# A two-layer hybrid block on one core: tokens loaded as feature columns, a later rate exponential, a scheduler that puts layer-norm steps first, and accumulating transfers for eight weight rows of the hybrid output

## The chip, the cores and the metric

The kernel runs on one core of one Trainium2 chip. The metric is device time in microseconds; the time of a kernel is the median of its runs. A profile shows one execution. The engines are TensorE (PE, with its weight loads as PEld), VectorE (DVE), ScalarE (ACT), GpSimd (POOL) and SyncE (SP), which here only issues transfers.

## What is computed

The input is one sequence of 256 tokens with 1024 features, all in float32. Six sublayers follow each other, each with a scaled residual (alpha is the square root of 2) and a layer norm: a feed-forward network, a hybrid mixer (a gated delta rule branch and a state-space branch side by side), two more feed-forward networks, a sparse attention mixer (NSA), and a last feed-forward network.

```python
def swiglu(x, w_in, w_out):
    gate, up = jnp.split(x @ w_in, 2, axis=-1)
    return (jax.nn.silu(gate) * up) @ w_out

def hybrid_mixer(x, w_in, ..., w_out):
    proj = x @ w_in
    ...
    o_a = gdn_branch(...)          # uses g = -exp(a_log) * softplus(a_logit + dt_bias)
    o_b = ssd_branch(...)          # uses a = -exp(a_log), dt = softplus(dt_logit + dt_bias)
    return jnp.concatenate([o_a, o_b], axis=-1) @ w_out
```

A feed-forward network goes from 1024 to twice 2816 features and back, with half its output added to the residual. The hybrid output multiplies 2048 features (16 rows of 128) by a 2048 x 1024 matrix.

## The kernel before

**Products of split operands.** Every large product is made from two parts per operand. A high part is the value rounded to the fast matmul type (fp32r), a low part is what is left. `split` writes the high part with a copy (ACT, or DVE where the planner chooses) and the low part with a subtraction on DVE. Three matmuls give high by high, high by low and low by high. A weight tile of 128 x 1024 (512 KB) is loaded by SP into a tile `raw` and split into `whi` and `wlo` (`arrive`, `halved`). Tokens are held as feature columns: `x[0]` is four tiles with high and low parts, each for two blocks of 128 features and both blocks of 128 tokens; `x[1]` keeps the unsplit columns, from which `token_forms` builds the sums for the wide products.

**Added rows.** `rows(w, f, added)` loads one row tile of an output matrix. With `added`, the low part is not subtracted on DVE: ACT writes minus the rounded value into `wlo`, and a transfer issued by POOL adds the weights from memory on top. Before the change, seven of the 22 rows of each feed-forward output (`ADDED`) are made in this way and none of the hybrid output.

**The planner.** All operations are first recorded in a `Plan` with tiles and data dependencies. `order` then simulates the engines with a price per operation and a latency per pair of engines, and picks at each step, for each engine, the operation that can start first; ties go to the lower priority number, which is the order of recording. It decides the order of the instructions on each engine, and through it which buffer is used when. On the chip, engines run their lists in order and wait only for data and buffers. A gate (`_Gate`, `late`) is a dependency for the planner alone. Every instruction is emitted by one helper, so all of them have line 561 in the profile, and groups are told apart by tiles. 52 tiles of 4 KB per partition hold everything in SBUF, with quotas by stream; `ORDER` adds fixed random offsets to the priorities of the NSA stage, drawn with a fixed number.

**The start.** `run` spins TensorE on a tile of ones, loads the token rows in four parts (`load`), transposes each part on TensorE in four blocks, copies the transposed part into `x[1]` and splits it into `x[0]` (`transpose_half`). Parts two to four are loaded and transposed between the weight tiles of `first_weights`, as `arrivals` say. `first_steps` then multiplies the first 512 gate features (four weight tiles, bank `acc`, 48 matmuls) and the first 512 up features (four tiles, bank `ps`, 48 matmuls). The loaded rows stay in `self.ah` as the residual.

**The hybrid stage.** `hybrid` loads its small parameters early, behind a gate. `rate`, the exponential of the decay parameters, is recorded after the copy of the projected logits and before the sigmoid; it depends only on its own small load. Five generators (`delta`, `space`, `gate`, `space2`, `out_a`) are woven together. `out_a` multiplies rows 0 to 7 of the output matrix, and rows 8 to 15 follow in `out_terms`, which takes the last `LAG` = 7 rows first for all of token block 0 and then for block 1, so that the norm of block 0 runs beside the products of block 1.

**Layer norm.** `layer_norm` adds the residual, takes the statistics, normalises in two halves, and transposes and splits each half for the next stage.

Of the kernel before, what the change touches and what calls it, by code (L numbers as in the profile page):

```python
# [10 lines left out]
F32R = mybir.dt.float32r  # L11
# [7 lines left out]
P = 128  # L19
# [31 lines left out]
CHUNKS, AHEAD, LAG = 4, 3, 7  # L51

TERMS = ((0, 1, 1, 1, 1, 1, 1), (0, 0, 1, 1, 1, 1, 0), (0, 0, 1, 1, 1, 1, 0), (0, 0, 1, 1, 1, 0, 0))

ADDED = range(8, 22, 2)
# [6 lines left out]
RANK = 0  # L62

# [118 lines left out]
class Op:  # L182
    __slots__ = ("eng", "fn", "args", "kw", "idx", "prio", "cost", "table", "deps", "succ", "ndep", "ready", "start",
                 "end", "alloc", "dense", "alts", "tiles", "nbytes", "quad", "port", "banks")


class Plan:
# [11 lines left out]
    def __init__(self):  # L199
        self.ops = []  # L200
        self.tiles = []
        self.base = 0
        self.gate = None
        for e in ("tensor", "vector", "scalar", "gpsimd", "sync"):
            setattr(self, e, _Eng(self, e))
# [7 lines left out]
    def add(self, eng, fn, args, kw, alts=None):  # L213
        op = Op()
        op.eng, op.fn, op.args, op.kw, op.idx = eng, fn, args, kw, len(self.ops)
        op.prio = op.idx + self.base
        op.alts = alts
        op.deps, op.succ, op.alloc, op.nbytes = {}, [], None, 0
# [133 lines left out]
    def order(self, caps):  # L352
# [27 lines left out]
        port = 0.0  # L380
# [67 lines left out]
        while left:  # L448
            best = None
            for e in engs:  # L450
# [6 lines left out]
                for op in lst:  # L457
# [24 lines left out]
            (key, op, pen), e = best  # L482
            st = key[0] + pen
# [23 lines left out]
            if fn == "dma_start":  # L507

                at, need = st + 1300, op.nbytes * (2 if e == "gpsimd" else 1)
                while need > 0:  # L510
                    n = int(at / 500)
                    room = (155e3 if at < 8000.0 else 190e3) - moved.get(n, 0)
                    take = min(need, room, room * (n + 1 - at / 500), 95e3 if e == "gpsimd" else need)
# [3 lines left out]
                op.end = at + 600  # L517
# [67 lines left out]
class K:  # L585
    NT = 2
# [130 lines left out]
    def first_weights(self, w, n0, arrivals):  # L717

        out = []
        for n in range(4):  # L720
            src = w[n0 + n]
            raw = self.m4(1024, "raw", "W")
            hi, lo = (self.m4(1024, name, "W", F32R) for name in ("whi", "wlo"))
            step = 512 if arrivals and n < 2 else 1024
            for e in range(0, 1024, step):
                cs = slice(e, e + step)
                self.nc.sync.dma_start(raw[:, cs], src[:, cs])
                self.split(hi[:, cs], lo[:, cs], raw[:, cs])
                for f in (arrivals.pop(0) if arrivals else []):
                    f()  # L730
            out += [(hi[:, k * 512:k * 512 + 512], lo[:, k * 512:k * 512 + 512]) for k in range(2)]
        return out
# [207 lines left out]
    def layer_norm(self, b, acc, s, gb, x, last):  # L940
# [70 lines left out]
    def first_steps(self, x, w_in, gtiles, gts):  # L1011
# [4 lines left out]
        for c0, tag, arrivals in ((0, "acc", self.arrivals), (DFF, "ps", [])):  # L1016
# [15 lines left out]
        for b in range(2):  # L1032
# [6 lines left out]
            for f in range(4):  # L1039
                self.split(gts[f][0][:, b * P:(b + 1) * P], gts[f][1][:, b * P:(b + 1) * P], pt[:, f * P:(f + 1) * P])  # L1040
            with _Gate(self.plan, len(self.plan.ops) - 1):
                self.scale_h(b)

    def ffn(self, l, j, x, then, last=False):
# [5 lines left out]
        NT = self.NT  # L1050
# [21 lines left out]
        else:  # L1072
# [4 lines left out]
            for b in range(2):  # L1077
                for s in range(NT):
                    ps = self.bank("ps")
# [28 lines left out]
        steps = NF // 2 - 2 * CHUNKS  # L1108
        for s in range(NT, steps):
            wg, wu = (self.col_tiles([w_in[8 + 4 * (s - NT) + 2 * n + e] for e in range(2)]) for n in range(2))  # L1110
# [14 lines left out]
        for n in range(CHUNKS):  # L1125
            f0 = 2 * steps + 4 * n
            gout = [self.m4(1024, name, "G", F32R).rearrange("p (f t) -> p f t", f=4) for name in ("gh", "gl")]
            part = self.wide(w_in, 8 + 4 * (steps - NT) + 8 * n, forms, gout)
            for most in TERMS[n]:
# [119 lines left out]
    def hybrid(self, x, then):  # L1249
# [430 lines left out]
        def out_a():  # L1680
# [3 lines left out]
            for s in range(4):  # L1684
                wo = [self.rows(w_out, 2 * s + e) for e in range(2)]
# [9 lines left out]
        for s in range(4):  # L1695
            wo = [self.rows(w_out, 8 + 2 * s + e) for e in range(2)]
# [406 lines left out]
    def run(self, stages):  # L2103
# [14 lines left out]
        spin(4, 2)  # L2118
        self.ah = [self.m4(D, f"h{b}", "L") for b in range(2)]

        def load(b, q):
            cs = slice(q * 512, (q + 1) * 512)
            nc.sync.dma_start(self.ah[b][:, cs], self.i['x'][0, b * P:(b + 1) * P, cs])
            self.transpose_half(x, b, self.ah[b], q)

        load(0, 0)
        with _Gate(self.plan, len(self.plan.ops) - 3):
            spin(2, 2)
        self.arrivals = [[], [lambda: load(1, 0)], [], [lambda: load(0, 1), lambda: load(1, 1)]]
# [45 lines left out]
_INS = ['x', 'positions', 'ln_g', 'ln_b', 'ffn_w_in', 'ffn_w_out', 'hyb_w_tok', 'hyb_w_col', 'hyb_w_small',  # L2175
# [5 lines left out]
def laid_out(inputs):  # L2181
# [4 lines left out]
    steps = DFF // 256 - 2 * CHUNKS  # L2186
    ffn = []
    for l in range(2):
        for j in range(2):
            w = a['ffn_w_in'][l, j]  # L2190
            g, u = w[:, :DFF], w[:, DFF:]
            if l + j == 0:
                t = [rows(g[:, :512], 2), rows(u[:, :512], 2)]
            else:
                t = [rows(np.concatenate([g[:, c:c + 256], u[:, c:c + 256]], 1), 2) for c in (0, 256)]
# [43 lines left out]
```

## Time and profile before

| | us |
|---|---|
| median of 3 runs | 1088.05 (1086.9 to 1091.03) |
| the profiled execution | 1087.19 |
| its span, first to last instruction | 1085.5 |
| ACT busy | 725.9 |
| POOL busy | 70.7 |

The span is cut in stages by the order of the sublayers. In the page's picture of 40 slices (27.1 us each; digits are tenths of busy time) the four lines that matter are these:

```profile
PE   8999999998999999999999999999999999999997
...
DVE  7999999799979999999999999999978889999995
ACT  7767866368737774667866667678465778666780
...
PEclk9999999999999999999999999999999899999999
DMA  8658768535433575367777736679563336457881
```

PE and DVE are full in nearly all slices, ACT at two thirds, the DMA engines at a half to three quarters. The granted clock of TensorE is full but for one slice in the NSA stage. Where an engine waited, and for what, is shown with the prediction.

### The profile page before, as it was taken

Reading aid. Unit: us, or ns where it says so; the run is one execution under the profiler, and the core shown is the slowest. Engines: PE = TensorE matmul, PEld = TensorE weight load, DVE = VectorE, ACT = ScalarE, POOL = GpSimd, SP = SyncE. Lnnn points to the kernel's source line nnn. Section 1 sums busy time; section 2 is a strip of 40 time slices with the busy share of each in tenths; the row PEclk is TensorE's granted clock in tenths of the full one; section 3 lists DMA queues with packets and bytes.
Section 4 is the critical chain, followed back from the end, with each engine's and each line's share of the span. In section 5 each row is a group of like instructions: output and inputs, shape, how many; then the busy total and the mean of one; then the engine's idle time right before and its main releaser. Section 6 shows DMA issues by size and latency. Waiting matters only on the chain.

```text
span 1085.5 us, 16212 instructions
## 1 busy us (share of the span) xinstructions
PE 1066.3 (98%) x5946; PEld 893.3 (82%) x5946; DVE 1010.9 (93%) x1453; ACT 725.9 (67%) x1155; POOL 70.7 (7%) x116
## 2 busy tenths in 40 slices
PE   8999999998999999999999999999999999999997
PEld 6788888897999788888888888888887778888886
DVE  7999999799979999999999999999978889999995
ACT  7767866368737774667866667678465778666780
POOL 1000000001001310000000000000001000000000
PEclk9999999999999999999999999999999899999999
DMA  8658768535433575367777736679563336457881
GB/s 330 231 196 256 221 233 284 179 135 182 140 115 99 194 269 180 117 230 251 215 229 254 257 125 215 235 241 303 189 214 98 92 123 216 152 188 236 255 231 41
DMA packets 65034, 215.71 MB, mean 199 GB/s; under 512 B 8301, under 2 KB 12218, under 8 KB 64954
## 3 DMA queue, kind: packets, MB, share of 16 engines
q1 hardware_dynamic: 60922, 199.98, 52.8%
q0 software_dynamic: 4032, 14.68, 7.2%
q8 instruction: 47, 0.77, 0.3%
q14 instruction: 33, 0.27, 0.1%
HBM read 211.86 MB, written 1.07 MB: 196 GB/s over the span
## 4 chain that ended last, share of the span: by engine, by line
PE 84%; DVE 12%; ACT 1%; DMA 1%; issue 1%; POOL 0%; SPq 0%; DVEq 0%; ACTq 0%
PE ps L561 39%; PE acc L561 31%; PE mp L561 14%; DVE wlo L561 2%; DVE cv L561 2%; DVE arena L561 1%; DMA raw<-in_ffn_w_in_dram 1%; DVE o L561 1%; DVE sw L561 1%; DVE x L561 1%; DVE y L561 1%; DVE qs L561 1%; DVE AT L561 0%; POOL arena L561 0%; DVE Y L561 0%
## 5 line engine op out<-in xcount | busy, mean ns | idle before, releaser
L561 ACT ACTIVATE whi<-raw 128x1024 fp32r<-128x1024 f32 (+1 forms) x435 | 436.8, 1052 | 104.0 <-DVE raw L561 85.4
L561 DVE TENSOR_TENSOR wlo<-raw,whi 128x1024 fp32r<-128x1024 f32 (+2 forms) x419 | 491.4, 1205 | 7.1 <-ACT whi L561 6.1
L561 PE MATMUL ps<-whi,x 128*128 128x512 f32 (+1 forms) x864 | 234.8, 390 | 0.3 <-ACT cv L561 0.3
L561 PEld LDWEIGHTS ps<-whi,x 128*128 128x128 f32 x864 | 156.7, 188 | 30.6 <-issue 1.5
L561 DVE TENSOR_TENSOR raw<-raw,raw 128x1024 f32<-128x1024 f32 x128 | 152.8, 1216 | 0.0
L561 PE MATMUL ps<-wlo,x 128*128 128x512 f32 (+1 forms) x432 | 127.1, 385 | 0.0
L561 PE MATMUL ps<-x,whi 128*128 128x256 f32 (+2 forms) x560 | 114.3, 312 | 4.0 <-ACT cv L561 2.4
L561 PEld LDWEIGHTS ps<-x,whi 128*128 128x128 f32 (+1 forms) x560 | 90.4, 188 | 11.4 <-ACT cv L561 3.8
L561 PE MATMUL acc<-whi,gh 128*128 128x512 f32 x253 | 99.3, 393 | 0.0
L561 PE MATMUL acc<-wlo,gh 128*128 128x512 f32 x253 | 99.0, 391 | 0.0
L561 PE MATMUL acc<-whi,gl 128*128 128x512 f32 x253 | 97.9, 390 | 0.0
L561 PEld LDWEIGHTS ps<-wlo,x 128*128 128x128 f32 x432 | 79.6, 188 | 15.3 <-issue 0.4
L561 PE MATMUL ps<-x,wlo 128*128 128x256 f32 (+1 forms) x344 | 80.0, 284 | 0.5 <-DVE wlo L561 0.5
L561 PE MATMUL acc<-whi,x 128*128 128x512 f32 x224 | 73.7, 405 | 2.3 <-DVE x L561 0.8
L561 PE MATMUL acc<-whi,g 128*128 128x512 f32 x192 | 63.3, 392 | 0.0
L561 POOL DMA_DIRECT2D wlo<-in_ffn_w_out_dram x28 | 24.4, 872 | 569.2 <-ACT wlo L561 391.3
L561 PEld LDWEIGHTS ps<-x,wlo 128*128 128x128 f32 (+1 forms) x344 | 58.1, 189 | 2.1 <-DVE wlo L561 0.7
L561 PEld LDWEIGHTS acc<-whi,gl 128*128 128x128 f32 x253 | 47.5, 188 | 9.8
L561 PEld LDWEIGHTS acc<-whi,gh 128*128 128x128 f32 x253 | 47.5, 188 | 9.5
L561 PEld LDWEIGHTS acc<-wlo,gh 128*128 128x128 f32 x253 | 47.5, 188 | 9.5
L561 PEld LDWEIGHTS acc<-whi,x 128*128 128x128 f32 x224 | 41.8, 189 | 11.8 <-ACT whi L561 2.1
L561 PE MATMUL mp<-whi,fhi 128*128 128x512 f32 x128 | 49.9, 390 | 0.0
(284 smaller groups left out, 1735.2 us busy)
## 6 DMA issues: line engine op xcount, KB each, us to landing
raw<-in_ffn_w_in_dram SPq DMA_DIRECT2D x174, 512.0 KB, 5.5
raw<-in_ffn_w_out_dram SPq DMA_DIRECT2D x88, 512.0 KB, 3.7
wlo<-in_ffn_w_out_dram POOLq DMA_DIRECT2D x28, 512.0 KB, 8.5
raw<-in_hyb_w_col_dram SPq DMA_DIRECT2D x28, 512.0 KB, 4.5
raw<-in_hyb_w_tok_dram SPq DMA_DIRECT2D x16, 512.0 KB, 7.8
raw<-in_hyb_w_out_dram SPq DMA_DIRECT2D x16, 512.0 KB, 3.7
raw<-in_nsa_w_tok_dram SPq DMA_DIRECT2D x8, 512.0 KB, 6.6
raw<-in_nsa_w_one_dram SPq DMA_DIRECT2D x8, 512.0 KB, 5.8
```

Source lines behind the costliest of these rows:

```text
L561: r = getattr(getattr(nc, eng), fn)(*[res(a) for a in args], **{k: res(a) for k, a in kw.items()})
```

## The change

Seven things change.

1. **Tokens as feature columns.** The host passes the tokens a second time, transposed, as `x_cols`: four tiles, each of 128 partitions (the features of a block) by two token blocks, two feature blocks and 128 tokens. `first_loads` issues a column tile before each of the first four weight tiles and then the other four weight tiles; the columns go straight into `x[1]` and are split from there. The transposes, their copies and `arrivals` go. The token rows for the residual are loaded later, behind a gate on the last of these loads.
2. **Spin.** Two spins of 512 columns at the start in place of one of 512 and three of 256, the last two of which were behind a gate.
3. **Late exponential.** `rate` is recorded after the sigmoid and gated on the sigmoid's exponential.
4. **Layer norm first.** Operations recorded inside `layer_norm` are marked `hot`; on DVE and ACT the planner compares them as if they could start 135 ns earlier than they can.
5. **Added rows in the hybrid output.** The eight even rows of 16 get their low part by a transfer.
6. **The planner's model of accumulating transfers.** They follow each other, move up to 130 instead of 95 KB per half microsecond, and end 500 ns later.
7. **Chunks per feed-forward network.** `CHUNKS` becomes a tuple, with code for a fifth chunk; all four values are 4, as before.

```diff
-CHUNKS, AHEAD, LAG = 4, 3, 7
+CHUNKS, AHEAD, LAG = (4, 4, 4, 4), 3, 7
...
-ADDED = range(8, 22, 2)
+ADDED, ADDED_HYB = range(8, 22, 2), range(0, 16, 2)
...
+HOT = 135.0
+
+ADD_RATE, ADD_LATE = 130e3, 500.0
...
-                    key = (st if st > f + 1e-9 else f, p)
+                    at = st - HOT if op.hot and e in ("vector", "scalar") else st
+                    key = (at if at > f + 1e-9 else f, p)
                     if cand is None or key < cand[0]:
-                        cand = (key, op, pen)
+                        cand = (key, op, pen, st)
...
-            (key, op, pen), e = best
-            st = key[0] + pen
+            (key, op, pen, st), e = best
+            st = max(st, free[e]) + pen
...
                 at, need = st + 1300, op.nbytes * (2 if e == "gpsimd" else 1)
+                if e == "gpsimd":
+                    at = max(at, adds)
...
-                    take = min(need, room, room * (n + 1 - at / 500), 95e3 if e == "gpsimd" else need)
+                    take = min(need, room, room * (n + 1 - at / 500), ADD_RATE if e == "gpsimd" else need)
...
-                op.end = at + 600
+                if e == "gpsimd":
+                    adds = at
+                op.end = at + 600 + (ADD_LATE if e == "gpsimd" else 0.0)
...
+    def first_loads(self, x, w):
+
+        nc = self.nc
+        raws = []
+        for n in range(8):
+            if n < 4:
+                nc.sync.dma_start(x[1][n // 2][:, :, n % 2 * 2:n % 2 * 2 + 2, :],
+                                  self.i['x_cols'][n].rearrange("p (b k t) -> p b k t", b=2, k=2))
             raw = self.m4(1024, "raw", "W")
...
+            for cs in [slice(0, 512), slice(512, 1024)] if n == 0 else [slice(0, 1024)]:
+                nc.sync.dma_start(raw[:, cs], w[n][:, cs])
+            raws.append(raw)
+        return raws
...
-    def layer_norm(self, b, acc, s, gb, x, last):
+    def layer_norm(self, *args):
+        self.plan.hot = True
+        self.normalize(*args)
+        self.plan.hot = False
+
+    def normalize(self, b, acc, s, gb, x, last):
...
-            w = self.first_weights(w_in, 4 if c0 else 0, arrivals)
+            w = []
+            for n in range(4):
+                if c0 == 0:
+                    hi, lo = (x[0][n][:, :, e] for e in range(2))
+                    self.split(hi, lo, x[1][n // 2][:, :, n % 2 * 2:n % 2 * 2 + 2, :].rearrange("p b k t -> p k b t"))
+                w += self.first_weights(raws.pop(0), [slice(0, 1024)] if c0 or n else [slice(0, 512), slice(512, 1024)])
...
+            with self.late():
+                nc.sync.dma_start(self.ah[b], self.i['x'][0, b * P:(b + 1) * P])
             with _Gate(self.plan, len(self.plan.ops) - 1):
                 self.scale_h(b)
...
-        nc.scalar.activation(rate, rate, AF.Exp)
         beta = self.sm([P, 2, 8], "beta")
         self.sigmoid(beta, sm[:, :, 0:8])
+        with _Gate(self.plan, len(self.plan.ops) - 3):
+            nc.scalar.activation(rate, rate, AF.Exp)
...
-                wo = [self.rows(w_out, 2 * s + e) for e in range(2)]
+                wo = [self.rows(w_out, 2 * s + e, 2 * s + e in ADDED_HYB) for e in range(2)]
...
-            wo = [self.rows(w_out, 8 + 2 * s + e) for e in range(2)]
+            wo = [self.rows(w_out, 8 + 2 * s + e, 8 + 2 * s + e in ADDED_HYB) for e in range(2)]
...
-        spin(4, 2)
+        spin(4, 4)
...
+    a['x_cols'] = a['x'].reshape(2, P, 4, 2, P).transpose(2, 4, 0, 3, 1).reshape(4, P, 512)
```

More of the change, by code (lines that the diff above doesn't have):

```diff
@@ L183 @@
     __slots__ = ("eng", "fn", "args", "kw", "idx", "prio", "cost", "table", "deps", "succ", "ndep", "ready", "start",
-                 "end", "alloc", "dense", "alts", "tiles", "nbytes", "quad", "port", "banks")
+                 "end", "alloc", "dense", "alts", "tiles", "nbytes", "quad", "port", "banks", "hot")
 class Plan:
@@ L217, in add @@
         op.alts = alts
+        op.hot = self.hot
         op.deps, op.succ, op.alloc, op.nbytes = {}, [], None, 0
@@ L379, in order @@
         partial = False
-        port = 0.0
+        port = adds = 0.0
         activity = {}
@@ L585 @@
 class K:
-    NT = 2
     def __init__(self, plan, ins, caps):
@@ L715, in rows, with first_weights @@
         return hi, lo
[L717 to L721, printed above, removed]
-            raw = self.m4(1024, "raw", "W")
[L723 to L732, printed above, removed]
+    def first_loads(self, x, w):
[5 more added lines that the diff above has]
+                                  self.i['x_cols'][n].rearrange("p (b k t) -> p b k t", b=2, k=2))
+            raw = self.m4(1024, "raw", "W")
+            for cs in [slice(0, 512), slice(512, 1024)] if n == 0 else [slice(0, 1024)]:
+                nc.sync.dma_start(raw[:, cs], w[n][:, cs])
+            raws.append(raw)
+        return raws
+    def first_weights(self, raw, parts):
+        hi, lo = (self.m4(1024, name, "W", F32R) for name in ("whi", "wlo"))
+        for cs in parts:
+            self.split(hi[:, cs], lo[:, cs], raw[:, cs])
+        return [(hi[:, k * 512:k * 512 + 512], lo[:, k * 512:k * 512 + 512]) for k in range(2)]
     def token_forms(self, x):
@@ L1015, in first_steps @@
         banks = []
-        for c0, tag, arrivals in ((0, "acc", self.arrivals), (DFF, "ps", [])):
+        raws = self.first_loads(x, w_in)
+        self.mark = len(self.plan.ops) - 1
+        for c0, tag in ((0, "acc"), (DFF, "ps")):
             both = [self.bank(tag) for b in range(2)]
             banks.append(both)
-            w = self.first_weights(w_in, 4 if c0 else 0, arrivals)
+            w = []
[4 more added lines that the diff above has]
+                w += self.first_weights(raws.pop(0), [slice(0, 1024)] if c0 or n else [slice(0, 512), slice(512, 1024)])
             for k0 in range(0, KD, 2):
@@ L1049, in ffn @@
         NF = DFF // P
-        NT = self.NT
+        CH = CHUNKS[2 * l + j]
+        NT = 2 if CH < 5 else 1
         pairs = {}
@@ L1078, in ffn @@
                 for s in range(NT):
-                    ps = self.bank("ps")
+                    ps = self.bank("ps" if NT > 1 else "acc")
                     self.proj_tok(x, b, steps[s], ps)
@@ L1107, in ffn @@
         terms += [(f, gts[f]) for f in range(2 * NT)]
-        steps = NF // 2 - 2 * CHUNKS
+        steps = NF // 2 - 2 * CH
+        if steps == NT:
+            forms = self.token_forms(x)
         for s in range(NT, steps):
-            wg, wu = (self.col_tiles([w_in[8 + 4 * (s - NT) + 2 * n + e] for e in range(2)]) for n in range(2))
+            wg, wu = (self.col_tiles([w_in[4 * NT + 4 * (s - NT) + 2 * n + e] for e in range(2)]) for n in range(2))
             self.mark = len(self.plan.ops) - 1
@@ L1124, in ffn @@
         weights_to(AHEAD)
-        for n in range(CHUNKS):
+        for n in range(CH):
             f0 = 2 * steps + 4 * n
             gout = [self.m4(1024, name, "G", F32R).rearrange("p (f t) -> p f t", f=4) for name in ("gh", "gl")]
-            part = self.wide(w_in, 8 + 4 * (steps - NT) + 8 * n, forms, gout)
-            for most in TERMS[n]:
+            part = self.wide(w_in, 4 * NT + 4 * (steps - NT) + 8 * n, forms, gout)
+            for most in TERMS[CH][n]:
                 next(part)
@@ L2117, in run @@
         nc.scalar.activation(tab, self.mhalf, AF.Silu)
-        spin(4, 2)
+        spin(4, 4)
         self.ah = [self.m4(D, f"h{b}", "L") for b in range(2)]
[L2121 to L2129, printed above, removed]
         self.marks = []
@@ L2191, in laid_out @@
             g, u = w[:, :DFF], w[:, DFF:]
+            CH = CHUNKS[2 * l + j]
+            steps = DFF // 256 - 2 * CH
             if l + j == 0:
@@ L2194, in laid_out @@
             else:
-                t = [rows(np.concatenate([g[:, c:c + 256], u[:, c:c + 256]], 1), 2) for c in (0, 256)]
+                t = [rows(np.concatenate([g[:, c:c + 256], u[:, c:c + 256]], 1), 2) for c in ((0, 256) if CH < 5 else (0,))]
             for c in range(512, steps * 256, 256):
```

7 lines of the change are left out of this document (4 added, 3 removed).

## The prediction

> **What bounds the kernel now.** I read the page's busy times and its chain first, then the waits of TensorE by stretch, then tables by window. In all rows of windows the columns are stretch and its length, busy us (instructions) of PE, PEld, DVE, ACT and POOL, granted clock, DMA share, GB/s.
>
> ```profile
> PE 1066.3 (98%) x5946; PEld 893.3 (82%) x5946; DVE 1010.9 (93%) x1453; ACT 725.9 (67%) x1155; POOL 70.7 (7%) x116
> ...
> PE 84%; DVE 12%; ACT 1%; DMA 1%; issue 1%; POOL 0%; SPq 0%; DVEq 0%; ACTq 0%
> ```
>
> TensorE is busy for 1066.3 of 1085.5 us. No edit takes a matmul of the model away (only 16 transposes of the tokens go), so the change can win little more than the 19 us in which PE stands still. Where those lie is told by PE's waits, first for the stretch 0 to 50 us, then 200 to 400, then 400 to 1070 (columns: total us, times, longest):
>
> ```profile
> PE ps L561 <- DVE sg L561: 1.6, 2, 1.1
> PE acc L561 <- POOL ones L561: 1.1, 1, 1.1
> PE acc L561 <- DVE x L561: 0.8, 2, 0.6
> PE acc L561 <- ACT whi L561: 0.8, 1, 0.8
> PE acc L561 <- ACT x L561: 0.5, 1, 0.5
> ...
> PE ps L561 <- ACT cv L561: 2.7, 3, 1.3
> PE ps L561 <- DVE wlo L561: 0.5, 1, 0.5
> ...
> PE mp L561 <- DVE arena L561: 1.3, 2, 0.8
> PE mp L561 <- ACT arena L561: 0.8, 1, 0.8
> ```
>
> So there are four places: the start, the convolutions of the hybrid stage (waits on cv), a short stretch of the NSA stage (arena), and the tail. The chain shows the start in order of time (start, us, what):
>
> ```profile
> 12.71 8.89 PE acc L561 x39
> 21.60 7.27 PE ps L561 x32
> ...
> 29.37 7.09 DMA raw<-in_ffn_w_in_dram
> ...
> 52.09 2.72 PE acc L561 x12
> ```
>
> Twelve dense matmuls take 2.72 us (last row). The first group of the first feed-forward stage (bank acc, 48 matmuls, 10.9 us of work) ends only at 21.6: 39 of its matmuls run without a break from 12.7, and before that PE spends its time on warm-up matmuls, transposes and waits. Its inputs come in like this:
>
> ```profile
> 0.00:3.00 3.00, 1.94 (x3) 0.90 (x4) 0.34 (x2) 1.49 (x2) 2.18 (x13) 1.00 0.34 110
> 3.00:6.00 3.00, 2.35 (x8) 1.37 (x6) 1.12 (x4) 0.63 (x1) 1.29 (x7) 1.00 0.80 257
> 6.00:9.00 3.00, 2.14 (x9) 1.62 (x9) 1.59 (x3) 1.11 (x2) 0.00 (x0) 1.00 1.01 311
> 9.00:12.00 3.00, 2.24 (x13) 1.54 (x12) 0.94 (x3) 2.12 (x6) 0.00 (x0) 1.00 1.03 417
> ...
> 24.00:27.00 3.00, 3.00 (x15) 2.49 (x14) 3.00 (x3) 2.05 (x3) 0.00 (x0) 1.00 0.78 229
> 27.00:30.00 3.00, 3.00 (x15) 2.49 (x14) 3.00 (x5) 2.48 (x3) 0.00 (x0) 1.00 0.37 50
> ```
>
> By these rates 0.33, 1.10, 2.03 and 3.28 MB have come by 3, 6, 9 and 12 us.
>
> **The change part by part.** *Tokens first.* The group needs 1 MB of tokens and 2 MB of weights before as after, so the bytes do not change; their use does. Before, nothing of a token quarter can be multiplied until rows have landed, four transposes have run and PSUM has been read. After, quarter n (0.26 MB) and weight tile n (0.52 MB) come in turn, and PE can do 12 matmuls with each pair. Pair n is complete at 0.79, 1.57, 2.36 and 3.15 MB, which by the rates above is about 4.8, 7.5, 9.8 and 11.7 us. What lies between landing and matmul:
>
> ```profile
> 4.41 0.63 ACT L561 ACTIVATE whi<-raw 128x512 fp32r<-128x512 f32 x1 [2.10 <-DMA raw<-in_ffn_w_in_dram]
> 6.22 0.68 DVE L561 TENSOR_TENSOR wlo<-raw,whi 128x512 fp32r<-128x512 f32 x1
> ...
> L561 ACT ACTIVATE whi<-raw 128x1024 fp32r<-128x1024 f32 (+1 forms) x435 | 436.8, 1052 | 104.0 <-DVE raw L561 85.4
> L561 DVE TENSOR_TENSOR wlo<-raw,whi 128x1024 fp32r<-128x1024 f32 (+2 forms) x419 | 491.4, 1205 | 7.1 <-ACT whi L561 6.1
> ```
>
> A pair costs ACT 0.63 + 1.05 = 1.7 us and DVE 0.68 + 1.21 = 1.9, both under PE's 2.72. With 1.05 for ACT's high part and about half a microsecond to land and hand over, pairs 1 to 3 can start at 9.1, 11.4 and 13.3 us. Pair 0 starts near 5.4, when ACT's first half at 4.41 is through (its end and the hand-over), and waits for its second half as before, to about 9. Then PE is the limit: 9.1, 11.8, 14.5, end 17.2. Against 21.6 that is **-4.4 us**. If loads never held it, 5.4 + 10.9 = 16.3 gives -5.3; if each pair came 1 us later, -3.4. The runs of the token tiles in SBUF are 1 KB; the nearest rows are the 4 KB rows at 417 GB/s above and, for 512-byte runs of zero fills,
>
> ```profile
> 264.00:265.00 1.00, 1.00 (x9) 1.00 (x10) 1.00 (x4) 1.00 (x1) 0.00 (x0) 1.00 1.02 284
> ```
>
> At 284 the megabyte takes 3.7 us where at 311 it takes 3.4: nothing.
>
> Does the gain last? The token rows are now loaded a second time for the residual: two more transfers on SP's queue behind the eight weight tiles, ahead of or among the next weights (1 MB, 2.5 us at 417). The DMA has 0.22 + 0.63 of 3 us free between 24 and 30, 2.6 us, and that covers it. The weights of the row 29.37 are issued as PE frees buffers, so they move up with PE. VectorE was idle for 8.0 of the first 12 us (rows above) and is full afterwards; it gains most of that. I keep -4.4, but -2 as the lower end, in case DVE moves up by less than PE. The spin matmuls fill time in which PE waits for data either way: nothing.
>
> *Late exponential.* In ACT's timeline (start, us):
>
> ```profile
> 31.55 1.28 ACT L561 ACT_TABLE_LOAD   x1
> ...
> 42.96 1.28 ACT L561 ACT_TABLE_LOAD   x1
> ```
>
> The rate's Exp switches the table inside a Silu stretch and back: 2.6 us of ACT go, and in the hybrid stage the Exp sits beside another. PE runs through both, with half a microsecond of the wait on sg near the second. I take -0.2, bounds 0 and -0.5.
>
> *Layer norm first.* The windows with the first boundary, then those where the hybrid's output rows are multiplied, then the NSA stretch:
>
> ```profile
> 160.00:180.00 20.00, 20.00 (x94) 16.64 (x93) 19.04 (x22) 16.39 (x19) 1.09 (x2) 1.00 1.00 327
> 180.00:200.00 20.00, 20.00 (x97) 16.34 (x96) 19.67 (x38) 7.24 (x15) 2.00 (x2) 1.00 0.60 218
> ...
> 360.00:380.00 20.00, 19.34 (x96) 15.03 (x96) 19.60 (x47) 14.84 (x30) 10.62 (x21) 1.00 0.71 238
> 380.00:400.00 20.00, 19.83 (x108) 16.26 (x107) 19.56 (x30) 13.45 (x26) 2.59 (x1) 1.00 0.76 266
> ...
> 840.00:860.00 20.00, 17.65 (x101) 13.71 (x98) 17.02 (x42) 16.47 (x57) 1.51 (x5) 0.83 0.18 61
> ```
>
> PE is at 20.00 of 20 across the boundary: half of the output matmuls hide the norm of the other half. The head start of 135 ns makes DVE wait at most that long, or lets a norm step pass a 1.2 us split. 0, bounds -1 and +0.5.
>
> *Eight added rows.* DVE loses 8 x 1.21 = 9.6 us, ACT gains 8 x 1.05 = 8.4, POOL 8 issues, the DMA 4 MB more. PE's idle time between 360 and 400 is 0.66 + 0.17 us, so the relief is worth at most 0.8; I take **-0.4**. The other side is the latency. Rows on loads (the additions' queue: packets, MB, share of the 16 engines; the landing of its 28 transfers; this stage's plain rows, with their landing; SP's issues of the last seven of them; and in the chain the matmuls with the second eight):
>
> ```profile
> q0 software_dynamic: 4032, 14.68, 7.2%
> ...
> DMA to landing us min/median/max: 5.4/8.5/11.2
> ...
> raw<-in_hyb_w_out_dram SPq DMA_DIRECT2D x16, 512.0 KB, 3.7
> ...
> 371.03 15.40 SPq L561 DMA_DIRECT2D raw<-in_hyb_w_out_dram  x7
> ...
> 396.38 7.07 PE acc L561 x31
> ```
>
> An added row needs 3.7 + 1.05 + about 1 (hand-over and issue) + 8.5 = 14.3 us from issue to use, a subtracted one 3.7 + 1.05 + 1.2 = 6. SP issues its last rows near 385. The matmuls with the second eight begin near 396, and by the order in out_terms the last added row is first used after 27 of them, 6 us later, 17 us after its issue: covered by 3 us. On POOL, which works in order, the additions stand between the stage's selections and powers (10.62 us busy from 360 to 380): a power behind an addition waits for ACT's copy, and the output norm of the branch waits for it. The 28 transfers hold the engines for 78 us, 2.8 each; eight more in the 40 us at 0.71 and 0.76 fill those to the brim. If that costs, up to +2.
>
> *New planner constants.* They reorder every stage. Idle that could be won: 3.2 us in the hybrid (cv and wlo), 2.4 in NSA, and 0.17 of the clock over 20 us there, 3.4; any of it can also double. I take 0, bounds -4 and +3. CHUNKS keeps the value 4 everywhere, so its new code changes nothing.
>
> Sum: -4.4 - 0.2 - 0.4 = -5.0. The profiled execution took 1087.19, its span 1085.5; the median of the runs is 1088.05, within 0.1%. 1087.2 - 5.0 = **1082.2 us**.
>
> [...] Loads and additions compete; a window among the first stage's last additions and one after them:
>
> ```profile
> 163.00:166.00 3.00, 3.00 (x15) 2.49 (x14) 3.00 (x4) 3.00 (x4) 0.00 (x0) 1.00 1.02 279
> ...
> 190.00:193.00 3.00, 3.00 (x15) 2.47 (x14) 2.96 (x6) 0.00 (x0) 0.37 (x1) 1.00 1.03 418
> ```
>
> Full engines move 279 instead of 418 GB/s. [...]
>
> **Rivals.** *DVE holds the start* (0.15): PE starts early but DVE, full from 12 us on, moves up by 2 only: 1085.2. For it: DVE is at 93%; against it: its 8 idle us at the start. *A worse redraw* (0.12): start as forecast, the new order adds 3 us in hybrid or NSA: 1085. *A better redraw* (0.20): 4 of the 9 us that lie there are won: 1078. *Late low parts* (0.08): PE, in order, stands at the second matmul of an added row. It decides when landing passes 11.5 us (8.5 plus the 3 of cover; the slowest now is 11.2); with rows 10, 12 and 14 each 3 us late, and as much again for the next stage's first weights, +12: 1094. That the change does nothing would need the first group to end at 21 us still; I give it no share of its own beyond the first rival.
>
> **How the numbers follow.** The forecast has 0.45. What a measurement can tell from no change is 0.5%, 5.4 us, so the border is 1082.6, just beside the forecast: I count two thirds of its 0.45 as faster, 0.29, and 0.16 as the same. Faster: 0.29 + 0.20 = 0.5; same: 0.16 + 0.15 + 0.11 = 0.42; slower: 0.08. The range runs from the better redraw with 2 more (1076) to the worse redraw and the first rival together (1088).
>
> **What would show it.** Right: bank acc's group ends near 17 us and ps's near 28, no mp<-ident,h before the first norm, 17 table loads instead of 19, 36 accumulating transfers, PE's idle time in 0 to 50 us down by over 2 us. Wrong: new waits of PE on wlo between 370 and 420, a DMA landing over 11.5 us there, a stretch of lower clock longer than 840 to 860, or a start that is won by 50 us and lost by 160.

## The result and the profile after

The changed kernel takes 1094.95 us (median of 6 runs, 1091.88 to 1096.65) against 1087.82 (6 runs, 1086.77 to 1091.03): a ratio of 1.0057, 95% interval 1.0044 to 1.0070. The forecast was 1082.2, and the range up to 1088 does not hold it. The profiled execution took 1092.94, its span 1091.0.

The page after, the busy line:

```profile
PE 1066.6 (98%) x5926; PEld 889.5 (82%) x5926; DVE 1010.0 (93%) x1441; ACT 731.0 (67%) x1153; POOL 74.0 (7%) x124
```

The queue of the adding transfers moves 18.88 MB, before 14.68. PE's work is as before within 0.3 us; the span is 5.5 us longer, so PE's idle time rose from 19.2 to 24.4 us. Windows of after, with the columns of the prediction:

```profile
6.00:9.00 3.00, 2.08 (x7) 1.35 (x6) 0.89 (x3) 1.26 (x2) 0.00 (x0) 0.76 0.98 319
9.00:12.00 3.00, 3.00 (x11) 2.29 (x10) 1.95 (x3) 2.09 (x3) 0.00 (x0) 0.67 1.04 405
24.00:27.00 3.00, 3.00 (x15) 2.49 (x14) 1.19 (x2) 3.00 (x6) 0.00 (x0) 1.00 1.04 408
...
120.00:140.00 20.00, 19.09 (x81) 14.78 (x80) 19.18 (x20) 18.04 (x21) 1.72 (x2) 1.00 0.84 255
160.00:180.00 20.00, 18.55 (x86) 15.07 (x85) 19.11 (x21) 17.87 (x22) 1.72 (x2) 1.00 1.04 343
...
380.00:400.00 20.00, 19.32 (x109) 15.93 (x108) 18.40 (x31) 17.13 (x31) 6.09 (x6) 1.00 0.97 305
```

Before, the window at 120 reads:

```profile
120.00:140.00 20.00, 20.00 (x90) 16.55 (x89) 19.79 (x20) 14.90 (x17) 0.86 (x1) 1.00 0.89 262
```

PE now stands still in places where it did not before: for 0.91 and 1.45 us in two windows of the first feed-forward stage (FFN 0 from here on), and for more than before in the hybrid's output. What it waited for, in the stretches 60 to 200, 340 to 440 and 540 to 640 us (total, times, longest):

```profile
PE acc L573 <- DMA wlo<-in_ffn_w_out_dram: 2.1, 2, 1.4
...
PE mp L573 <- DVE arena L573: 1.1, 1, 1.1
PE mp L573 <- DVE G L573: 1.0, 2, 0.7
PE acc L573 <- DMA wlo<-in_hyb_w_out_dram: 0.9, 1, 0.9
...
PE mp L573 <- DVE h L573: 0.8, 1, 0.8
```

The start itself is won, but less than forecast. The table gives starts of the same instructions in each profile's timeline, in us: the first matmul of bank `ps`, VectorE's `vg<-mp,vg` of the second wide product, GpSimd's power in the second norm of FFN 0 and of the hybrid, and the span. Single profiles of one order differ by some 2 us at the start (e2 and e3 begin with the order of before, and their bank `ps` starts at 23.4 and 23.2), so only larger differences count.

| kernel | ps | vg | norm FFN 0 | norm hybrid | span |
|---|---|---|---|---|---|
| before | 21.43 | 97.88 | 192.63 | 429.93 | 1085.5 |
| after | 19.20 | 97.77 | 192.01 | 430.69 | 1091.0 |
| e1 tokens first alone | 18.90 | 98.12 | 196.07 | 434.94 | 1091.0 |
| e6 e1, rows later | 18.82 | 93.81 | 192.43 | 435.90 | 1093.1 |
| e13 e6, tail tile | 18.77 | 93.80 | 189.76 | 429.59 | 1086.1 |
| e8, e12 neutral | 22.7, 22.9 | 98.3, 98.5 | 193.2, 193.2 | 434.3, 435.1 | 1091.6, 1090.9 |
| e15 neutral | 20.46 | 97.98 | 192.73 | 429.78 | 1087.4 |
| e16 all three mends | 19.55 | 95.04 | 190.99 | 427.21 | 1083.5 |

The norm columns of after can't be compared with the other rows, since its edit pulls the norm's steps ahead. By the median over the starts of matmuls of the same name and number, after is 3.7 us ahead of before between 50 and 95 us, 1.4 behind at 190 to 200, 4.6 behind at 440 and 5.7 behind at 600 to 640. So it loses in three places: most of it in FFN 0, some 3 us in the hybrid stage and 1 at the end of FFN 1.

In after PE is 2.2 us earlier at 20 us, hardly more than that spread, and 3.7 at 45 (the first wide product starts at 42.8 against 46.5), but VectorE's `vg` is not: 97.77 against 97.88. VectorE's row before:

```profile
97.88 0.68 DVE L561 TENSOR_TENSOR vg<-mp,vg 128x512 f32<-128x512 f32 x1
```

And after, from the timelines of SP, ACT and DVE:

```profile
10.13 1.68 SPq L573 DMA_DIRECT2D h<-in_x_dram  x2
12.21 4.16 SPq L573 DMA_DIRECT2D raw<-in_ffn_w_in_dram  x4
...
23.62 2.18 ACT L573 ACTIVATE h<-h 128x512 f32<-128x512 f32 x4
25.70 3.89 ACT L573 ACTIVATE whi<-raw 128x1024 fp32r<-128x1024 f32 x4
...
26.78 2.36 DVE L573 TENSOR_TENSOR wlo<-raw,whi 128x1024 fp32r<-128x1024 f32 x2 [1.81 <-ACT whi L573]
...
97.77 0.68 DVE L573 TENSOR_TENSOR vg<-mp,vg 128x512 f32<-128x512 f32 x1
```

The two token-row transfers stand on SP ahead of the next four weight tiles, and their four scalings on ACT ahead of these tiles' high parts (before, the scalings were gated on the last split and ran at 39 us). VectorE starves behind them: 1.19 of 3 us in the window at 24, where before it had 3.00. Up to `vg` it has 2.5 us less work than before (85.7 us against 88.2) and 2.4 us more idle time (12.1 against 9.6).

In after, GpSimd's seven adding transfers of FFN 0 wait for VectorE (3 times, 134.7 us) or ACT (4 times, 24.9 us) and not for PE. Two of them:

```profile
122.64 0.86 POOL L573 DMA_DIRECT2D wlo<-in_ffn_w_out_dram  x1 [24.31 <-DVE wlo L573]
...
155.41 0.86 POOL L573 DMA_DIRECT2D wlo<-in_ffn_w_out_dram  x1 [24.80 <-DVE wlo L573]
```

They are issued 3.5 and 3.2 us later than before (119.14 and 152.26), and PE's two waits on low parts in FFN 0 end 6.8 and 7.6 us behind them, at 129.5 and 163.0.

### The profile page after: what moved, and what is told of

Read it like the earlier page. It is cut to its first block, busy times and chain, and to the rows that moved or that the text cites. A ratio compares the mean times of both kernels' runs of the same rounds, so it can differ in the third digit from the quotient of the medians.

```text
span 1091.0 us, 16171 instructions
## 1 busy us (share of the span) xinstructions
PE 1066.6 (98%) x5926; PEld 889.5 (82%) x5926; DVE 1010.0 (93%) x1441; ACT 731.0 (67%) x1153; POOL 74.0 (7%) x124
## 3 DMA queue, kind: packets, MB, share of 16 engines
q0 software_dynamic: 5184, 18.88, 9.4%
## 5 line engine op out<-in xcount | busy, mean ns | idle before, releaser
L573 ACT ACTIVATE whi<-raw 128x1024 fp32r<-128x1024 f32 (+2 forms) x432 | 433.4, 1050 | 110.3 <-DVE raw L573 83.5
L573 DVE TENSOR_TENSOR wlo<-raw,whi 128x1024 fp32r<-128x1024 f32 (+2 forms) x410 | 482.7, 1208 | 11.8 <-ACT whi L573 10.8
L573 PE MATMUL ps<-wlo,x 128*128 128x512 f32 (+1 forms) x432 | 130.1, 389 | 0.0
L573 PE MATMUL acc<-whi,gh 128*128 128x512 f32 x253 | 97.1, 391 | 0.0
L573 POOL DMA_DIRECT2D wlo<-in_ffn_w_out_dram x28 | 24.4, 870 | 592.1 <-ACT wlo L573 397.0
L573 PEld LDWEIGHTS acc<-wlo,gh 128*128 128x128 f32 x253 | 47.5, 188 | 12.6 <-DMA wlo<-in_ffn_w_out_dram 3.0
L573 PE MATMUL ps<-whi,fhi 128*128 128x512 f32 x128 | 50.1, 391 | 0.3
```

The source lines that it names most:

```text
L573: r = getattr(getattr(nc, eng), fn)(*[res(a) for a in args], **{k: res(a) for k, a in kw.items()})
```

## The experiments

All are made from the two kernels, with five rounds each; a ratio is against the kernel before in the same rounds, with its 95% interval.

**Each part alone.** e1 has the new start (first_loads, first_steps, two spins of four), e2 the eight added rows, e3 the layer-norm preference, e4 the constants of the adding transfers, e7 the late exponential.

```diff
 # e1
-        spin(4, 2)
+        spin(4, 4)
...
+        raws = self.first_loads(x, w_in)
 # e2
-                wo = [self.rows(w_out, 2 * s + e) for e in range(2)]
+                wo = [self.rows(w_out, 2 * s + e, 2 * s + e in ADDED_HYB) for e in range(2)]
 # e3
+HOT = 135.0
 # e4
-ADD_RATE, ADD_LATE = 95e3, 0.0
+ADD_RATE, ADD_LATE = 130e3, 500.0
...
-                    at = max(at, 0.0)
+                    at = max(at, adds)
 # e7
+        with _Gate(self.plan, len(self.plan.ops) - 3):
+            nc.scalar.activation(rate, rate, AF.Exp)
```

> The kernel before with the tokens as feature columns, the new spin and the token rows loaded later; nothing else of the change. Theory A (the start is the cause: VectorE holds the first feed-forward stage): PE is ahead by about 3 us at 50 us, VectorE is idle for at least 11 us of the first 60 (9.6 before), PE waits for late low parts between 60 and 200 us, and the total is 1087 to 1090, no faster than before. Theory B (the loss comes from the new constants for accumulating transfers, which make additions come late in this stage): without them the 3 us stay, 1084 to 1085.

> The kernel before with the eight added rows in the hybrid output alone. Theory A: the additions fill the DMA between 360 and 420 us and cost about 2.7 us of PE there, as in the changed kernel: 1090 to 1091. Theory B (the late additions come from the new constants): with the old, slower model the planner asks for them earlier, PE does not wait for them, 1087 to 1088.

> The kernel before with the head start of 135 ns for layer-norm steps alone. If the parts add up, PE has no idle time at the boundaries to lose, and the time is 1087 to 1089. If any reordering of this plan costs time (the order before being a good draw), it is above 1089 with losses far from the norms.

> The kernel before with the new constants for accumulating transfers alone. Theory A: additions in the feed-forward stages keep a lead of over 10 us, nothing changes, 1087 to 1089. Theory B: in the first feed-forward stage additions are used at the moment they land, PE waits for them by 2 us or more, 1089 to 1091.

> The kernel before with the late rate exponential alone. My sum gave it -0.2 us (two table loads of 1.28 us go on an engine with slack). All theories: 1087 to 1088.5. Theory E alone allows up to 1091, since the new order differs from the old in many places though the step costs nothing.

| | us | ratio |
|---|---|---|
| e1 tokens first | 1093.35 | 1.0048 (1.0031 to 1.0065) |
| e2 added rows | 1091.19 | 1.0026 (1.0013 to 1.0040) |
| e3 layer norm first | 1090.76 | 1.0020 (1.0007 to 1.0033) |
| e4 constants | 1087.85 | 1.0000 (0.9987 to 1.0013) |
| e7 late exponential | 1088.77 | 1.0009 (1.0000 to 1.0018) |

Theory B (the constants) falls with e4, and so does theory A's price for e1. The largest loss alone is that of tokens first; the parts alone add up to +12.6 us (differences of medians) where the whole has +7.1, so they are not independent. e2's time is what theory A gave, but not for its reason: PE's waits between 340 and 440 are as in the rows of after shown above (arena 1.1, G 1.0), and none is on a low part. What the added rows cost alone is VectorE's values in the new order, not their landing (median 8.4 us, slowest 11.6). In e3, the last wide product of FFN 1 shows how an order costs time (timelines of ACT and DVE):

```profile
582.73 1.06 ACT L573 ACTIVATE whi<-raw 128x1024 fp32r<-128x1024 f32 x1 [1.64 <-DMA raw<-in_ffn_w_in_dram]
...
583.82 1.23 DVE L573 TENSOR_TENSOR wlo<-raw,whi 128x1024 fp32r<-128x1024 f32 x1 [2.00 <-ACT whi L573]
584.97 0.68 DVE L573 TENSOR_TENSOR vg<-su,vg 128x512 f32<-128x512 f32 x1
```

A high part of the next stage now stands ahead of what `vg` needs. Its weights have not landed, ACT stands 1.64 us, VectorE 2.00 behind it, and PE waits 1.5 us for `vg`; before, PE had no wait there.

**What takes the start's gain back.** e1 falls behind between 93 and 105 us. Timelines of PE and DVE, then windows:

```profile
92.33 5.87 DVE L573 TENSOR_TENSOR wlo<-raw,whi 128x1024 fp32r<-128x1024 f32 x5 [0.57 <-ACT whi L573]
98.12 0.68 DVE L573 TENSOR_TENSOR vg<-mp,vg 128x512 f32<-128x512 f32 x1
98.72 0.50 PE L573 MATMUL acc<-wlo,gh 128*128 128x512 f32 x1 [1.92 <-DMA wlo<-in_ffn_w_out_dram]
```

```profile
96.00:99.00 3.00, 1.08 (x5) 0.62 (x4) 3.00 (x4) 3.00 (x5) 0.86 (x1) 1.00 1.04 306
99.00:102.00 3.00, 3.00 (x9) 2.35 (x9) 3.00 (x3) 3.00 (x4) 0.00 (x0) 0.54 1.07 381
102.00:105.00 3.00, 3.00 (x14) 2.43 (x13) 0.94 (x3) 3.00 (x4) 0.00 (x0) 0.89 0.61 120
```

PE waits 1.92 us for an added low part, and then the granted clock is low for two windows. e5 tests the transfer as the cause, e6 the token rows, which it puts behind the first block of the second wide product (in e6 they are issued at 58.5 us and scaled from 71.4 on, not at the 80 that the expectation says).

```diff
 # e5, on e1
-ADD_RATE, ADD_LATE = 95e3, 0.0
+ADD_RATE, ADD_LATE = 95e3, 3500.0
 # e6, on e1: the row loads and scale_h leave first_steps
+                if rows and n == 1 and most == 0:
+                    gate = max(o.idx for o in self.plan.ops if o.fn == "dma_start")
+                    for b in range(2):
+                        with _Gate(self.plan, gate):
+                            nc.sync.dma_start(self.ah[b], self.i['x'][0, b * P:(b + 1) * P])
+                        self.scale_h(b)
```

> e1_tokens (tokens first alone) with one constant changed: the planner counts an adding transfer as landed 3.5 us later than it did, so that the order puts its first user later. Theory C (tokens first wins 3.8 us by 50 us, but the PE order then reaches the first added row tiles of FFN 0 only 6 to 8 us after their adding transfers are issued, and these land 7.8 us after issue: the wait of 2.08 us at 98.7 us, the low clock behind it and the later ones are that): 1088 to 1090 us, at least 3.5 us under the 1093.35 of e1_tokens, and no PE wait on wlo from in_ffn_w_out. Theory D (the second load of the tokens and the scaling of them hold the start): unchanged start, 1092 to 1094. Theory E (any new order of the planner loses 2 to 4 us against this one): 1089 to 1093, without a link to wlo.

> e1_tokens with the second token load (two transfers of 512 KB) and the four scalings of it moved from the start to behind the first wide product's second block, about 80 us in. Theory D: the first 50 us get shorter by 1 to 2.5 us against e1_tokens (its PE idle there and DVE idle between 20 and 40 us go down; DVE was busy 16.57 of 20 us there against 18.80 before), and at least 1 us of that stays to the end: 1090 to 1092. Theory C: the start gets shorter, and the added row tiles of FFN 0 are reached earlier still, so the waits on wlo take it back: 1092.5 to 1094.5. Theory E: 1090 to 1095, without a link to either.

e5 took 1097.86 us, 1.0096 (1.0082 to 1.0109). Its PE has no wait on these low parts, and stands at the same place for as long:

```profile
98.35 0.68 DVE L573 TENSOR_TENSOR vg<-mp,vg 128x512 f32<-128x512 f32 x1
...
99.09 0.50 PE L573 MATMUL mp<-whi,fhi 128*128 128x512 f32 x1 [2.04 <-DVE vg L573]
```

So the transfer only stood in front of VectorE, which was no earlier: theory C falls. e6 took 1093.36, 1.0050 (1.0037 to 1.0062), but its profile tells more than its time. The window from 20 to 30 us of e1 and then of e6, and VectorE's `vg` in e6:

```profile
20.00:30.00 10.00, 9.94 (x44) 7.88 (x42) 7.23 (x8) 8.57 (x12) 0.00 (x0) 1.00 0.89 336
```

```profile
20.00:30.00 10.00, 9.87 (x44) 7.84 (x42) 9.78 (x10) 9.12 (x11) 0.00 (x0) 1.00 0.76 252
...
93.81 0.68 DVE L573 TENSOR_TENSOR vg<-mp,vg 128x512 f32<-128x512 f32 x1
```

VectorE works 2.6 us more in that window and reaches `vg` 4.3 us earlier; the same two adding transfers are issued 2 us earlier than before (117.14 and 149.95), and PE's lead of about 4 us lasts to 165 us. My reading in theory D that the start itself gets shorter was wrong (`ps` at 18.82 and 18.90). The lead is lost at two later places: some 4 us at the end of FFN 0 and some 4 in the hybrid stage. e9 and e10 carry the mend on: e9 is the whole change with e6's edit, e10 is e6 with e4's and e7's edits.

> The whole change with the second token load and its four scalings moved to about 80 us, as in e6_rows. Theory F (the rows' load and scaling ahead of the second weight tiles cost VectorE about 4 us of idle time before the first wide product's vg, so that PE's lead of 3.7 us meets a VectorE that is no earlier than before): vg near 94 us instead of 97.8, the lead of PE stays at 3.5 us or more up to 140 us. The hybrid layer's and the FFN 1 boundary's losses (about 3 and 1 us) stay: 1089 to 1093, against the 1094.95 of the change. Theory E (each new order is a draw of 0 to +4 us around the kernel before): 1087 to 1093 wherever vg falls.

> Tokens first with the rows moved, the late exponential and the new constants of the adding transfers, without the layer-norm preference and without the eight added row tiles. Theory F: vg near 94 us and a lead of 3.5 us up to 160 us; with no loss behind it the time is 1084 to 1086; with e6's waits at the end of FFN 0 and in the hybrid layer it is up to 1092. Theory E: 1084 to 1092, since a lead of 3.9 us and a draw of 0 to +4 us and more add up.

e9: 1096.69, 1.0082 (1.0069 to 1.0096). e10: 1093.97, 1.0066 (1.0051 to 1.0082). Both missed. `vg` moves as theory F says in e10 (93.90) and by less in e9 (95.95), and both lose it again: e9, like after, is 1.4 us behind before at 190 us. So on the whole change the move of the rows alone mends nothing. In e9's hybrid output the added rows are the largest wait, which is the mechanism of my slower rival:

```profile
PE acc L573 <- DMA wlo<-in_hyb_w_out_dram: 4.8, 3, 2.4
```

**The end of FFN 0.** In e6, PE's waits from 170 to 190 us:

```profile
PE acc L573 <- DMA wlo<-in_ffn_w_out_dram: 1.8, 1, 1.8
...
```

The last adding transfer is issued at 167.81 and lands after 9.6 us, at 177.4, among eight weight loads of the hybrid stage. e11 (e6 and e5 together) makes the planner count it as later; e13, on e6, moves it away by adding tiles 6 to 18 of FFN 0 instead of 8 to 20.

```diff
-                wos.append(self.rows(w_out, len(wos), len(wos) in ADDED))
+                wos.append(self.rows(w_out, len(wos), len(wos) in (range(6, 20, 2) if l + j == 0 else ADDED)))
```

> e6_rows with the planner counting an adding transfer as landed 3.5 us later, as in e5_addlate. Theory F with the waits on late low parts as a second cause (e6 lost 2.0 us at 177.4 us on wlo, whose adding transfers had only 2.7 to 7 us): the lead of 3.9 us now lasts to the end of FFN 0 (190 us), no PE wait on wlo from in_ffn_w_out; 1084 to 1090 depending on the order of the hybrid layer. Theory E: 1085 to 1093.

> e6_rows with one edit in FFN 0 alone: the adding transfers build the low parts of the row tiles 6 to 18 instead of 8 to 20, so that the last one is out of the time when eight weight transfers of the next layer run (e6 waited 2.0 us at 177.4 us for the last added tile, and the granted clock fell to 0.72 and 0.85 behind it). Theory G (FFN 0's last loss is that transfer's place): the lead of 3.9 us of e6 at 165 us is still over 2 us at 190 us, where e6 was 1.9 us behind the kernel before; no wait on wlo from in_ffn_w_out; the hybrid layer still has the form with the 4.28 us power instruction on GpSimd and loses 4.5 us: 1087.5 to 1090. If it is VectorE that ends FFN 0 (e11, without the wait, stood 5.4 us for h), it stays at 1092 to 1096.

e11: 1097.73, 1.0090 (1.0078 to 1.0102), a miss. No low part is late, but the new order puts seven splits for the next stage ahead of the norm, on which PE then stands (DVE's timeline, PE's wait):

```profile
172.85 8.04 DVE L573 TENSOR_TENSOR wlo<-raw,whi 128x1024 fp32r<-128x1024 f32 x7
180.79 0.69 DVE L573 SCALAR_TENSOR_TENSOR h<-acc,h 128x512 f32<-128x512 f32 x1
```

```profile
PE mp L573 <- DVE h L573: 5.3, 1, 5.3
```

e13: 1088.02, 1.0010 (1.0001 to 1.0019), 5.3 us under e6 (4.4 by the ratios) and as theory G said. e6 and e13 at that place:

```profile
176.00:180.00 4.00, 2.59 (x7) 2.07 (x8) 1.15 (x2) 2.35 (x3) 0.00 (x0) 0.72 0.39 152
180.00:184.00 4.00, 4.00 (x17) 3.23 (x16) 3.10 (x6) 0.82 (x1) 0.00 (x0) 0.85 0.00 0
```

```profile
176.00:180.00 4.00, 4.00 (x20) 3.30 (x19) 4.00 (x9) 1.24 (x2) 0.69 (x1) 1.00 0.00 0
```

The lead is still 2.9 us at the norm (189.76). It is then lost in the hybrid stage.

**Does any new order lose?** Three neutral redraws of the kernel before, by a constant that changes no work:

```diff
-                lat = 400.0 if fn == "dma_start" else self.latency(op, eng, s.eng)
+                lat = 410.0 if fn == "dma_start" else self.latency(op, eng, s.eng)   # e8; 390 in e12; 420 in e15
```

> The kernel before with one neutral constant of the planner changed (the lag that it adds behind a DMA's end, 400 ns to 410 ns), which redraws the order of some 5100 of 7200 listed PE rows from about 45 us on and changes no work. Theory E (the order of before is a good draw, and a new draw costs 2 to 4 us whatever the edit): 1089.5 to 1092. Theories C and D (each part's loss has a wait of its own behind it): within 1 us of before, 1087 to 1089.

> A second neutral redraw of the kernel before: the lag behind a DMA's end 390 ns instead of 400 ns (e8 had 410). Theory E: again slower by 1 to 4 us, 1089 to 1092, with waits of PE on VectorE in the hybrid layer, where e8 lost 3.9 us. If redraws are harmless as e4's was: 1087 to 1088.5.

> A third neutral redraw of the kernel before: the same lag at 420 ns, where the order on GpSimd in the hybrid layer is that of the kernel before (e8 at 410 ns and e12 at 390 ns had the other and lost 4 to 5 us). Theory H: 1087 to 1088.5. If any redraw costs: 1090 to 1093.

e8: 1091.88, 1.0040 (1.0027 to 1.0054). e12: 1092.73, 1.0048 (1.0036 to 1.0061). By the starts of the same matmuls both lose 4 to 5 us between 340 and 440, as do e5, e6, e10, e11 and e13, and all seven have one local order in common. e8 (GpSimd, VectorE, PE), then the same power before:

```profile
375.60 4.28 POOL L573 TENSOR_TENSOR arena<-arena,mhalf 128x8 f32<-128x8 f32 x1 [8.08 <-DVE arena L573]
...
379.92 1.04 DVE L573 TENSOR_TENSOR arena<-arena 128x8 f32<-128x8 f32 x1 [1.54 <-POOL arena L573]
...
384.31 0.49 PE L573 MATMUL mp<-bcT 128*128 128x128 f32 x2 [2.30 <-DVE y L573]
```

```profile
371.17 2.55 POOL L561 TENSOR_TENSOR arena<-arena,mhalf 128x8 f32<-128x8 f32 x1 [1.73 <-DVE arena L561]
```

In these seven GpSimd runs one of the two selections on G before this power, the power comes some 4 us later and takes 4.28 to 4.29 us; VectorE stands 1.54 us behind it, and PE 2.3 behind VectorE. (In after, e2 and e9 a selection stands ahead of the power too and it comes some 5 us later, but it takes 1.68, 1.68 and 2.58 us; so the selection alone does not make it long. The last section comes back to this.) e15 was picked since its order there is that of before: 1088.09, 1.0010 (0.9999 to 1.0020), with a power of 2.56 us. e14 is e6 with such an order (the constant at 390):

> e6_rows with the planner's lag behind a DMA's end at 390 ns, a neutral constant, chosen since GpSimd then runs the power instruction ahead of both selections on G in the hybrid layer, as in the kernel before (the six kernels that have lost 4 to 5 us there run one selection first, and their power instruction took 4.28 us against 1.68 to 2.58 in the others). Theory H (that order is the hybrid layer's loss): no loss over 1 us between 350 and 440 us; with e6's loss at the end of FFN 0, 1088 to 1090. If new orders lose wherever they differ: 1091 to 1094.

e14: 1089.69, 1.0025 (1.0012 to 1.0038), 3.7 us under e6 (2.7 by the ratios), with about 1 us lost in the hybrid stage. Theory E in its plain form (any new order loses) falls with e4 and e15. Theory H was drawn from e8 and e12 and held in e14 and e15. These orders differ from each other elsewhere too, and no run changed GpSimd's order alone.

**All three mends.** e16 is e13 with the late exponential, the new constants and `table_pen = 600` instead of 400, which gives GpSimd's order of before. e17 has two of its edits (`table_pen`, tiles 6 to 18) on the kernel before, and e18 is the whole change with the three mends: rows later, tiles 6 to 18, `table_pen` 600.

```diff
-    table_pen = 400
+    table_pen = 600
```

> Tokens first with the rows moved (e6), the added tiles of FFN 0 at 6 to 18 (e13), the late exponential, the new constants of the adding transfers, and the planner's penalty for a table load at 600 instead of 400, with which GpSimd's order in the hybrid layer is that of the kernel before; without the layer-norm preference and the added hybrid rows. Theories F, G and H together: the lead of 3.9 us from 50 us on is kept: 1083.5 to 1086, faster than the kernel before. If one of them fails: 1087 to 1091.

> The control for e16: the kernel before (tokens as rows, old start) with e16's other two edits, the added tiles of FFN 0 at 6 to 18 and the table penalty 600. If e16's 3.6 us come from tokens first (theories F, G, H): 1086.5 to 1089, no faster than the kernel before. If they come from these two edits by themselves: 1083 to 1085.

> The whole change with e16's three edits: e16 plus the layer-norm preference (e3 alone: +2.9 us) and the eight added hybrid rows (e2 alone: +3.3 us). If these two cost by themselves as they did alone: 1087 to 1091. If their losses were only the draw of the order: 1083 to 1086.

| | us | ratio |
|---|---|---|
| e16 | 1083.81 | 0.9970 (0.9959 to 0.9981) |
| e17 | 1088.42 | 1.0006 (0.9997 to 1.0015) |
| e18 | 1085.81 | 0.9989 (0.9979 to 0.9999) |

e16 beats both kernels: 3.6 us under before, and not by its other edits, since e17 gains nothing, nor do the constants and the late exponential alone (e4, e7). By the starts of the same matmuls it is 2.6 to 3.6 us ahead of before from 50 us on up to 640. Its PE stands still neither at the end of FFN 0 nor in the hybrid's output:

```profile
160.00:180.00 20.00, 20.00 (x93) 16.51 (x92) 20.00 (x25) 15.36 (x18) 0.00 (x0) 1.00 0.76 265
...
380.00:400.00 20.00, 19.99 (x103) 16.38 (x102) 19.56 (x28) 15.21 (x27) 4.05 (x2) 1.00 0.81 277
```

The layer-norm preference and the added hybrid rows cost about 2.0 us on top (e18 less e16), where alone they had cost 2.9 and 3.3; this lies in the second range that I had expected for e18, 1083 to 1086. They save VectorE 4.8 us (1006.6 busy against 1011.4) and PE does not profit: e18's PE waits 1.5 us for h at the FFN 1 boundary and 1.2 for G in the hybrid stage, where e16 has neither. Still e18 is 3.4 us ahead of before at 190 us, where after and e9 are 1.4 behind.

## Why the prediction was wrong

- **Tokens first, -4.4.** The start was won, though less: `ps` starts at 19.2 and not 17.2. PE waited 1.7 us for `whi`, and its clock was 0.76 and 0.67 between 6 and 12 us, where before had 1.00. That is not the whole of the 2 us: e1, with 0.6 us of these waits and the full clock, starts `ps` at 18.90. Whether the new spin had a part in the low clock is open; e1, e6 and e16 have the same spin and 1.00 there.
- **"Does the gain last?" is the step that failed.** I covered the second token load with 2.6 us of free DMA between 24 and 30. It was issued at 10 us, behind the eight weight tiles as I had put it and ahead of the next four, and I had not followed what else moves with it: the gate of `scale_h` refers to the operation recorded last, which is now the row load, so the scalings ran ahead of the high parts. And I let VectorE move up with PE, by most of the 8 us that it was idle in the first 12. It is idle there for 7.5 us after the change too (busy for 0.35, 1.32, 0.89 and 1.95 of 3 us each), since the high parts that it needs wait for columns and weights to land (it waits 6.0 us for ACT's high parts there, and ACT 5.1 us for these loads). VectorE and PE are nearly full between 50 and 120 us; with `vg` no earlier and the adding transfers 3 us later, PE's lead had nowhere to go. My lower end of -2 and the rival "DVE holds the start" (1085.2) name the engine, but give up only half of the gain; the lead was spent entirely. e6 shows the step: row load and scalings away, `vg` 4.3 us earlier, lead kept to 165 us. On the whole change that was not enough by itself (e9); with the two other mends the lead lasts there too (e18). Which of the two moves matters more was not tried apart. The size of the term was not far off: with the lead kept, e16 is 3.6 us under before.
- **Later in FFN 0** PE met the adding transfers: in after because they were issued later than before (2.1 us of waits), in e6 because PE was early at the last one (1.8 us; e13 takes it away). That is my rival "late low parts" at another place than I put it. In the hybrid's output, where I put it, the slowest landing was 11.0 us, under the 11.5 that I gave as the border, and PE waited 0.9.
- **Eight added rows, -0.4 with up to +2:** +3.3 alone (e2), outside the bounds; **layer norm first, 0 with up to +0.5:** +2.9 alone (e3), outside too. Both through the order that they draw: with the mends, they cost +2.0 together. I had excluded it for the norm by saying that PE is full across the boundary. That is true of the order before, and the edit makes another.
- **Planner constants, 0:** right (e4), and the **late exponential** is too small to tell from nothing (e7). Its table loads fell from 19 to 17 alone, but in the changed kernel there are 19: ACT's new order put two back.
- **The redraw.** I priced it as +3 at worst and as an alternative beside a start that is kept (1085 us, 0.12). Neutral redraws gave +4.0, +5.5 and +0.7 us, and the lost start came on top. The signs that I had written down as wrong (a start won by 50 us and lost by 160, new waits on wlo) are those that came; of the signs of being right, PE's idle time in the first 50 us fell by 1.7 us, not by over 2.

## What to carry to other kernels

When two engines are both full, an earlier start of one is worth what the other can follow (here PE's lead of 3.7 us at 45 us was gone by 190 us with `vg` at 97.77, in after, and one of about 4 us lasted to 165 us with `vg` at 93.81, in e6): find the first value that the full engine needs from the other, and read its time, not the time of the first matmul. When a load moves, list with it every instruction gated on it and everything behind it on its queue and on the engine that uses it. Where a planner orders the work, run a redraw that changes nothing as a control before a few microseconds are put down to an edit, and compare local orders to find the one that loses.

## What the hardware showed

**A stall can cost more than its length.** After PE's stalls of 1.8 to 2.5 us in e1, e5, e6 and e10, the clock's rows miss the same amount: in e1 0.46 + 0.11 and in e5 0.31 + 0.26 of 3 us, in e6 0.28 + 0.15 and in e10 0.29 + 0.14 of 4, each 1.7 us. After the 5.3 us in e11 it is twice that:

```profile
184.00:188.00 4.00, 0.00 (x0) 0.00 (x0) 4.00 (x9) 0.00 (x0) 1.01 (x1) 0.91 0.96 362
188.00:192.00 4.00, 3.55 (x13) 3.10 (x14) 3.96 (x12) 1.81 (x4) 0.55 (x1) 0.50 0.35 143
192.00:196.00 4.00, 4.00 (x16) 3.18 (x15) 2.63 (x4) 0.00 (x0) 0.00 (x0) 0.73 0.11 9
```

The missing 0.09 + 0.50 + 0.27 of 4 us is 3.4 us, though part of it lies in the stall itself. After 1.4 us in after and 2.3 in e8, the clock stayed at 1.00 (162 to 168 us in after, 382 to 388 in e8). So in these profiles the length of a stall alone does not tell whether the clock falls behind it, and no run shows what else does.

**A power on GpSimd has no fixed price.** The same 128x8 power took 1.68 to 2.58 us in most profiles and 4.28 or 4.29 in the seven of one order. In e8 it is issued at 375.60, and VectorE runs a split, a copy and a product from SBUF until 378.38:

```profile
375.43 1.21 DVE L573 TENSOR_TENSOR wlo<-raw,whi 128x1024 fp32r<-128x1024 f32 x1
...
377.17 1.21 DVE L573 TENSOR_TENSOR G<-G,arena 128x1024 f32<-128x1024 f32 x1
```

Without the 2.78 us of overlap with these, 1.50 us of the power are left. Before, it overlaps the end of a split for 1.05 us and takes 2.55, which leaves 1.50 too; in e9 it is 1.04 of 2.58, and in after, where VectorE's products and copies meanwhile read PSUM and a split overlaps only the last 0.15 us, the power takes 1.68. In the fourteen profiles of before, after and e1 to e12, 1.50 to 1.54 us are left when the overlap with VectorE's wide instructions that read SBUF alone is taken off. That the power stands still beside these is my reading of the overlaps; no run here took these instructions apart.
